# Prompt head norms in 32 rows per pair of heads beside the samples' first key group, and the prompt half of the output projection queued behind the second group's keys

## The chip, the cores and the metric

The kernel runs on one core of a Trainium2 chip. The core has a matrix engine (TensorE, PE in the profile; its weight loads are shown apart as PEld), a vector engine (VectorE, DVE), a scalar engine with function tables (ScalarE, ACT), a general engine (GpSimd, POOL) and an engine that only issues transfers (SyncE, SP). Each takes the instructions of its own queue in order and waits on semaphores for the others. TensorE writes to eight PSUM banks of 128 partitions by 512 floats; VectorE and ScalarE read them. The metric is device time of one execution in microseconds, the median of several runs.

## The reference

One step of a hybrid decoder layer for a prompt of 512 tokens and a group of 32 sample tokens (8 sequences of 4) that share the weights. The part that matters here is the end of the attention branch and the output projection:

```python
h = rmsnorm(x, w['g_mix'])
(q, kc_new, vc_new, ks_new, vs_new, kw_new, vw_new, g_nsa, xm, vm, om, i_pre, f_pre) = split_cols(h @ w['w_in'])
k_cmp = compress(kc_all, *w['cmp_k'])        # caches of 2048 tokens per sample, blocks of 32, stride 16
v_cmp = compress(vc_all, *w['cmp_v'])
o_nsa = nsa_attend(q, k_cmp, v_cmp, ks_all, vs_all, kw_all, vw_all, gates, offset, w_pre)
#   = gate0 * compressed attention + gate1 * attention over the 16 selected blocks + gate2 * window attention
o_nsa = rmsnorm(o_nsa, w['g_head_nsa'])      # over the 64 values of each of the 8 heads
hm = rmsnorm(mlstm_chunked(...), w['g_head_m']) * sigmoid(om)
mix = jnp.concatenate([o_nsa, hm], axis=-1) @ w['w_out']     # 1024 x 1024
x = x + mix
# then cross attention, SwiGLU and the final norm
```

A head norm is `y * rsqrt(mean(y*y) + 1e-6) * g`.

## The kernel before

All activations are held transposed, features on partitions and tokens on columns: 544 columns, first 512 of the prompt and then 32 of the samples. Dense products run over two column halves, `hf` 0 (columns 0 to 271) and 1 (272 to 543), so half 0 holds prompt tokens only and half 1 the rest of the prompt and all samples. A number in full precision is split into a rounded high part (ScalarE, line 213) and a remainder (VectorE or GpSimd, line 214), and a product is three matmuls (lines 218 to 220).

`oF` is [128, 8, 544]. Blocks 0 to 3 hold the attention output, two heads of 64 rows each per block; blocks 4 to 7 the mLSTM output. Once the projection's operands are split out of it, `oF` becomes `xT`, the residual stream, into which the input rows are transposed (`load_xT`, line 1811; lines 1817 and 206 or 208 in the profile).

Around the change the work comes from generators. A background generator (`compress(1)`, the compression of the values) is woven with a foreground chain `fg`: mLSTM, then `sample()`, then `open_late()`. Each step that a generator yields costs some credit, and the weave hands the other side a step when the credit is there. This sets only the order in which instructions are written down. A planner then places them on the engines' queues: it plays the program with a priced cost for each instruction, takes what is ready, and prefers what was written first. `tc.issue_after(ins)` adds an edge: the instructions of its block that run on the engine of `ins` are put behind `ins` on that engine.

`sample()` handles the samples in two groups `g` of four sequences. For each group it does the window attention; then, again for both groups, the selected keys: the compressed scores `weigh` and the choice of blocks `select`, four steps `c` in which gathered rows are turned by `keys()` (four transposes on TensorE, line 1518, and one copy by `evac`, line 206 or 208), then multiplied with the queries (`quad`, line 1528) and biased (line 1671), then the exponentials (lines 1701 and 1703). After both groups' keys come the selected values (line 1722), group 0, then group 1. The rows are gathered by indirect transfers that GpSimd issues (line 573), into eight buffers `gat`, so a gather waits until the buffer's last reader is through.

Between the values of group 0 and group 1 stands `finals_p` (line 1391), the end of the prompt's attention. For each of four blocks j it adds the compressed branch (line 1398 on TensorE, 1401 on VectorE), squares (1402, ScalarE), forms the mean over 64 rows by a product with the constant `bones` (128 x 128, two diagonal blocks of 1/64; line 1407), which leaves each mean in all 64 rows, and copies it (1408). Then one Ln (1411) and one Exp (1412) run over 128 x 2048 numbers and give the inverse root, and four VectorE instructions (1415) scale `oF`.

`finals_s` (line 1745) closes the samples; `open_late` (line 1777) splits columns 272 to 543 of `oF` for the projection (tiles `hh`, `hl`), and after the whole chain `fg` is drained, `early_mix` (line 1824) splits columns 0 to 271 (tiles `mh`, `ml`) and transposes the input rows. Only then the projection is written down (lines 1951 to 1960): half 0 with the weights' column chunks 0 and 1, then 2 and 3 (the chunks' split, `split_w`, is lines 213 and 214, tiles `whi`, `wlo`), and half 1 with chunks 2, 3, 0, 1. Chunks 0 and 1 are loaded early, one of them into a `cgat` buffer; chunks 2 and 3 pass through one `wraw` buffer (lines 1861 and 1863 on SP); chunks 0 and 1 are loaded again for half 1 into the pool `wp`, which takes over the space that `sample()` leaves. Of PSUM, the pools `psp` and `ppo` have one bank each, `ptp` and `pbd` two, `pxa` and `pxc` one.

## Time and profile before

| | |
|---|---|
| median of 3 runs | 1232.87 us (1231.31 to 1234.45) |
| profiled execution | 1243.24 us |
| its span, first to last instruction | 1241.5 us |
| TensorE busy | 1174.3 us (95%) |
| VectorE busy | 841.2 us (68%) |
| ScalarE busy | 612.4 us (49%) |
| GpSimd busy | 558.6 us (45%) |
| mean granted TensorE clock | 0.974 of full speed |
| sum of squares of the prompt's first block, line 1402 | starts at 566.5 us |
| prompt's Ln and Exp, lines 1411 and 1412 | 581.1 and 585.4 us |
| scalings, line 1415 | 587.3 to 590.1 us |

The profile is of one execution; its times count from the span's start. A row of groups gives line, engine, operation, output and input, shape, count, busy time and mean duration in nanoseconds, and the idle time before with what ended it. A row of windows gives, for a stretch, the busy time of each engine with its instructions, the granted clock, the share of the transfer engines and GB/s. A row of the chain gives start, duration and the work that was last to end at that point. Busy time of TensorE includes the latency of matmuls that overlap with nothing.

### The profile page before, as it was taken

The numbers are of one execution on the slowest core, as the hardware profiler recorded it, in microseconds if no ns is written. First come the engines' busy times: TensorE is split into PE (matmuls) and PEld (weight loads), VectorE is DVE, ScalarE is ACT, GpSimd is POOL, SyncE is SP. The second block draws the span as 40 slices with busy tenths as digits, with TensorE's granted clock in tenths as the row PEclk, the third lists the DMA queues.
The fourth block names the chain that finished last, engine by engine and source line by source line (L and its number), as shares of the span: only waits on it lengthen the run. The fifth ranks groups of instructions, "written<-read, shape, count | busy, mean of one in ns | idle before, by whom it ended". The sixth has DMA issues, their size and how long they took to land.

```text
span 1241.5 us, 24581 instructions
## 1 busy us (share of the span) xinstructions
PE 1174.3 (95%) x9220; PEld 1066.7 (86%) x9220; DVE 841.2 (68%) x1901; ACT 612.4 (49%) x1414; POOL 558.6 (45%) x686
## 2 busy tenths in 40 slices
PE   7999999899997989988999989999899999999996
PEld 5998999588885878854999987599899999999996
DVE  6337683567787687653754756554998888888874
ACT  5235665745545444466542423342665565555452
POOL 1013353566666266542342100043885576476342
PEclk9999999899997999999999998999999999999998
DMA  7324240141253185566767298630032333322411
GB/s 232 102 53 105 86 153 1 51 137 44 78 171 115 42 283 176 178 227 205 206 135 171 83 239 288 231 128 2 1 119 86 103 96 107 106 94 77 137 52 73
DMA packets 141769, 154.30 MB, mean 124 GB/s; under 512 B 17449, under 2 KB 123689, under 8 KB 141394
## 3 DMA queue, kind: packets, MB, share of 16 engines
q1 hardware_dynamic: 131922, 119.17, 32.0%
q0 software_dynamic: 9728, 33.56, 8.3%
q8 instruction: 73, 1.20, 0.4%
q14 instruction: 46, 0.38, 0.1%
HBM read 141.67 MB, written 13.12 MB: 125 GB/s over the span
## 4 chain that ended last, share of the span: by engine, by line
PE 49%; DVE 8%; ACT 3%; DMA 2%; issue 2%; SPq 1%; POOL 1%; POOLq 0%; DVEq 0%; ACTq 0%
PE xc L2291 7%; PE xa L2291 7%; PE bd L2291 5%; PE tp L2291 5%; PE bd L220 3%; PE bd L219 3%; PE bd L218 3%; DVE sp L2231 1%; DMA mkv<-in_cache_mem_k 1%; PE xa L1296 1%; PE tp L1518 1%; PE bd L2190 1%; PE xa L218 1%; PE xa L219 1%; PE xa L220 1%
## 5 line engine op out<-in xcount | busy, mean ns | idle before, releaser
L214 POOL TENSOR_TENSOR al<-fraw,ah 128x512 fp32r<-128x512 f32 (+1 forms) x104 | 127.5, 1227 | 152.4 <-ACT ah L213 124.0
L213 ACT ACTIVATE whi<-wraw 128x1024 fp32r<-128x1024 f32 (+3 forms) x74 | 62.5, 890 | 57.5 <-DMA wraw<-in_w_xv 28.2
L214 DVE TENSOR_TENSOR wlo<-wraw,whi 128x1024 fp32r<-128x1024 f32 (+3 forms) x74 | 73.6, 1026 | 19.1 <-ACT whi L213 19.0
L213 ACT ACTIVATE ah<-fraw 128x512 fp32r<-128x512 f32 (+1 forms) x112 | 65.8, 593 | 38.0 <-PE xc L2291 11.8
L218 PE MATMUL bd<-w1h,xh 128*128 128x256 f32 x256 | 82.6, 325 | 0.9 <-issue 0.9
L220 PE MATMUL bd<-w1h,xl 128*128 128x256 f32 x256 | 75.6, 298 | 3.0 <-DVE xl L214 3.0
L1198 POOL TENSOR_TENSOR xs<-xf 128x256 f32<-128x256 f32 x64 | 55.8, 878 | 50.2 <-PE xa L1296 30.5
L219 PE MATMUL bd<-w1l,xh 128*128 128x256 f32 x256 | 75.7, 297 | 0.0
L1296 PE MATMUL xa<-ws,xs 128*128 128x256 f32 x256 | 71.2, 400 | 2.4 <-DVE bq L1470 1.3
L625 POOL TENSOR_SCALAR sb<-sb,rs,gat 128x128 f32<-128x128 f32 (+3 forms) x64 | 46.1, 724 | 54.4 <-DVE rs L624 40.2
L213 ACT ACTIVATE xh<-xf 128x512 fp32r<-128x512 f32 x64 | 40.0, 629 | 45.5 <-DVE xf L1191 20.0
L213 ACT ACTIVATE ah<-sp 128x512 fp32r<-128x512 f32 (+1 forms) x64 | 35.5, 555 | 50.1 <-DVE sp L2231 22.8
L220 PEld LDWEIGHTS bd<-w1h,xl 128*128 128x128 f32 x256 | 48.9, 192 | 6.4 <-DVE xl L214 3.8
L1296 PEld LDWEIGHTS xa<-ws,xs 128*128 128x128 f32 x256 | 46.5, 201 | 8.5 <-issue 2.9
L218 PEld LDWEIGHTS bd<-w1h,xh 128*128 128x128 f32 x256 | 49.1, 193 | 5.0 <-issue 3.9
L214 DVE TENSOR_TENSOR xl<-xf,xh 128x512 fp32r<-128x512 f32 x64 | 47.5, 746 | 8.6 <-ACT xh L213 7.7
L219 PEld LDWEIGHTS bd<-w1l,xh 128*128 128x128 f32 x256 | 49.4, 193 | 4.5 <-issue 2.8
L219 PE MATMUL bd<-hlo,whi 128*128 128x272 f32 x176 | 52.0, 296 | 0.0
L218 PE MATMUL bd<-hhi,whi 128*128 128x272 f32 x176 | 51.7, 294 | 0.0
L1191 DVE STREAM_TRANSPOSE xf<-cgat 128x512 f32<-128x512 f32 x64 | 44.7, 703 | 10.2 <-POOL xs L1198 8.4
L220 PE MATMUL bd<-hhi,wlo 128*128 128x272 f32 x176 | 51.3, 292 | 0.0
L2231 DVE TENSOR_TENSOR sp<-fraw 128x512 f32<-128x512 f32 (+1 forms) x32 | 47.8, 1494 | 0.2
(990 smaller groups left out, 4667.9 us busy)
## 6 DMA issues: line engine op xcount, KB each, us to landing
fraw<-in_w_gate SPq DMA_DIRECT2D x11, 1024.0 KB
fraw<-in_w_up SPq DMA_DIRECT2D x11, 1024.0 KB
fraw<-in_w_down SPq DMA_DIRECT2D x24, 384.0 KB
mkv<-in_cache_mem_k SPq DMA_DIRECT2D x64, 128.0 KB
mkv<-in_cache_mem_v SPq DMA_DIRECT2D x16, 512.0 KB
wraw<-in_w_in SPq DMA_DIRECT2D x8, 512.0 KB
wraw<-in_w_xq SPq DMA_DIRECT2D x4, 1024.0 KB
wraw<-in_w_xk SPq DMA_DIRECT2D x4, 1024.0 KB
```

Of the source, the lines that this page charges most:

```text
L213: nc.scalar.activation(hi, src, AF.Copy)
L214: (eng or nc.gpsimd).tensor_tensor(lo, src, hi, op=OP.subtract)
L218: nc.tensor.matmul(out, ah, bh, start=first, stop=False, **kw)
L219: nc.tensor.matmul(out, ah, bl, start=False, stop=False, **kw)
L220: nc.tensor.matmul(out, al, bh, start=False, stop=last, **kw)
L625: (nc.vector, nc.gpsimd)[1].tensor_scalar(sb[:, :n], sb[:, :n], rs, gat[:, i, 3 * h + 1 + br:3 * h + 2 + br], op0=OP.mult, op1=OP.mult)
L1191: nc.vector.transpose(xf.rearrange("p a (q i) -> p q a i", q=4), gs[0].rearrange("p (q t a i) -> p t q a i", q=4, t=4, a=4)[:, t])
L1198: nc.gpsimd.tensor_tensor(xs_.rearrange("p c (v j) -> p v c j", v=2), xg[:, 0], xg[:, 1], op=OP.add)
L1296: nc.tensor.matmul(dst[2], ops[2][:, kk], w1s[t][2][:, kk], start=t == 0 and kk == 0, stop=t == 3 and kk == 1, skip_group_check=True)
L1518: nc.tensor.transpose(p[:, 128 * i:128 * i + 128], srcs(i), ident)
L2231: nc.vector.tensor_tensor(o, a, b, op=op)
L2291: nc.tensor.matmul(p[:, :HALF], w[a][:, k], x[b_][:, k], start=first and k == 0 and i == 0, stop=last and k == n - 1 and i == 2, skip_grou ...
```

## The change

`finals_p` gets a different form and a different place. Its sum of squares uses every fourth column of `bones`, so one block's result is 32 rows (16 equal rows for each of two heads) in place of 128; the four blocks stand in the four row groups of one 128 x 512 tile, and Ln and Exp run over that tile once. A matrix `spread` (formed by four small products of the same columns with the identity, and scaled by 4) brings each block's 32 rows back to 128 by a product of 32 rows, and the scaling reads that product from PSUM. The 32 rows are copied by VectorE, not ScalarE. All its PSUM banks come from the pool `ppo`. For scratch it uses `r3`, a tile of the compression's pool, the tile `SW` of the window attention, and a new tile `GX`.

The generator `fp` of it is advanced two steps after every two keys, in the first group's loop, and run to its end after that group's exponentials; the loop of the second group has the same extra yields with nothing left to do. The place between the two groups' values is gone.

`keys()` can mark its copy: the fourth key of each of the second group's steps 0, 1 and 2 is then copied by ScalarE and kept in a list `cgs["kt"]`. `early_mix` is written down before the chain `fg` is drained, with its splits behind the second mark on ScalarE; it transposes the row tiles 0 to 2 (columns 0 to 271). The split of the weights' chunks 0 and 1 stands behind the third mark. The row tiles 3 to 5 (the other columns) are transposed beside the second pair of chunks, and the loads of tiles 4 and 5 stand behind the last load of a weight chunk on SP. Row tiles 0 to 2 use only the bank of `psp`, as `ppo` is in use by the values. The pool `wp` is opened after the chain, as before.

```diff
--- before.py
+++ after.py
@@ -1388,32 +1388,36 @@
                     nc.scalar.activation(PcT[:, :, 128 * i - 128:128 * i], p[:, :256].rearrange("p (v t) -> p v t", v=2), AF.Copy)
                 yield
 
-        def finals_p(var):
+        def finals_p(sq, vt, spread):
             yield from need(("p", 1))
-            var = var[:, :2048].rearrange("p (a b n) -> p a b n", a=2, b=2)
-            for j in range(5):
-                if j < 4:
-                    acc = bank(psp)
-                    for v in range(2):
-                        nc.tensor.matmul(acc[64 * v:64 * v + 64], vcP[32 * j:32 * j + 32, v], PcT[32 * j:32 * j + 32, v],
-                                         start=True, stop=True)
-                    oj = oF[:, j, :512]
-                    nc.vector.tensor_tensor(oj, oj, acc, op=OP.add)
-                    nc.scalar.activation(var[:, j // 2, j % 2], oj, AF.Square)
-                    yield
-                if j > 0:
-                    p = bank(ptp)
-                    vj = var[:, (j - 1) // 2, (j - 1) % 2]
-                    nc.tensor.matmul(p, bones, vj, start=True, stop=True)
-                    nc.scalar.activation(vj, p, AF.Copy)
-                if j < 4:
-                    yield
-            nc.scalar.activation(var, var, AF.Ln, bias=eps_t)
-            nc.scalar.activation(var, var, AF.Exp, scale=-0.5)
+            p = bank(ppo)
             for j in range(4):
-                oj, vj = oF[:, j, :512], var[:, j // 2, j % 2]
-                nc.vector.scalar_tensor_tensor(oj, oj, gh[:, j:j + 1], vj, op0=OP.mult, op1=OP.mult)
-            yield
+                nc.tensor.matmul(p[32 * j:32 * j + 32, :128], bones[:, 0:128:4], ident, start=True, stop=True)
+            nc.scalar.activation(spread, p[:, :128], AF.Copy, scale=4.0)
+            yield
+            for j in range(4):
+                js = slice(32 * j, 32 * j + 32)
+                acc = bank(ppo)
+                for v in range(2):
+                    nc.tensor.matmul(acc[64 * v:64 * v + 64], vcP[js, v], PcT[js, v], start=True, stop=True)
+                oj = oF[:, j, :512]
+                nc.vector.tensor_tensor(oj, oj, acc, op=OP.add)
+                nc.scalar.activation(sq, oj, AF.Square)
+                yield
+                p = bank(ppo)
+                nc.tensor.matmul(p[js], bones[:, 0:128:4], sq, start=True, stop=True)
+                nc.vector.tensor_copy(vt[js], p[js])
+                yield
+            nc.scalar.activation(vt, vt, AF.Ln, bias=eps_t)
+            nc.scalar.activation(vt, vt, AF.Exp, scale=-0.5)
+            yield
+            for j in range(4):
+                js = slice(32 * j, 32 * j + 32)
+                p = bank(ppo)
+                nc.tensor.matmul(p, spread[js], vt[js], start=True, stop=True)
+                oj = oF[:, j, :512]
+                nc.vector.scalar_tensor_tensor(oj, oj, gh[:, j:j + 1], p, op0=OP.mult, op1=OP.mult)
+                yield
 
         def sample():
             yield from need(("w", 1))
@@ -1518,9 +1522,12 @@
                     nc.tensor.transpose(p[:, 128 * i:128 * i + 128], srcs(i), ident)
                 return p
 
-            def keys(srcs):
+            def keys(srcs, mark=False):
                 kt_ = sc.tile([128, 512], F32, name="kt", bufs=4)
-                evac(kt_, four_t(srcs))
+                if mark:
+                    cgs["kt"].append(nc.scalar.activation(kt_, four_t(srcs), AF.Copy))
+                else:
+                    evac(kt_, four_t(srcs))
                 return kt_
 
             def quad(S, bs, keys_of):
@@ -1536,6 +1543,7 @@
                 evac(PT_, four_t(srcs).rearrange("p (i r) -> p i r", i=4))
                 return PT_
 
+            cgs["kt"] = []
             win = {(0, "k"): kwin(0), (0, "v"): vwin(0), (1, "k"): kwin(1)}
             yield 2
             for g in range(2):
@@ -1638,6 +1646,7 @@
                 nc.vector.tensor_scalar(mk[:, 1:31], ia, -0.5 * BIG, BIG, op0=OP.is_ge, op1=OP.mult)
                 sel[g] = mk
 
+            fp = finals_p(r3, sc.tile([128, 544], F32, name="SW")[:, :512], sc.tile([128, 128], F32, name="GX"))
             G, st_ = {}, {}
             G[0, "k0"] = half("cache_k_slc", 0, 0)
             G[0, "k1"] = half("cache_k_slc", 0, 1, range(3))
@@ -1676,9 +1685,11 @@
                     kts = []
                     for q in range(4):
                         c0 = 512 * ((c + 1) % 2)
-                        kts.append(keys(lambda i: src[q][:, c0 + 128 * i:c0 + 128 * i + 128]))
+                        kts.append(keys(lambda i: src[q][:, c0 + 128 * i:c0 + 128 * i + 128], g == 1 and q == 3))
                         if q % 2:
                             yield
+                            yield next(fp, None)
+                            next(fp, None)
                     if g == 0 and c > 0:
                         (weigh, select)[c - 1](1)
                     if c == 2:
@@ -1704,6 +1715,8 @@
                 nc.vector.tensor_reduce(rs[:, 1:2], bs5[:, 5:10], axis=AX.X, op=OP.add)
                 st_[g] = SS, rs
                 yield
+                if g == 0:
+                    yield from fp
             for g in range(2):
                 SS, rs = st_[g]
                 if g:
@@ -1737,8 +1750,6 @@
                 nc.vector.tensor_tensor(rs[:, 2:3], rs[:, 2:3], g3[:, g, 1:2], op=OP.mult)
                 nc.vector.scalar_tensor_tensor(ocs[:, g], po_[:, 0:128], rs[:, 2:3], ocs[:, g], op0=OP.mult, op1=OP.add)
                 yield
-                if g == 0:
-                    yield from finals_p(sc.tile([128, 2080], F32, name="SS", bufs=2))
             pop("sc")
             pop("mixS")
 
@@ -1812,23 +1823,26 @@
             t0, n = xtl[i]
             x = xts[i]
             for c in range(2):
-                p = rot(psp, ppo)
+                p = bank(psp) if i < 3 else rot(psp, ppo)
                 for k in range(4):
                     nc.tensor.transpose(p[:, n * k:n * k + n], x[:n, 512 * c + 128 * k:512 * c + 128 * k + 128], ident[:n, :n])
                 evac(xT[:, 4 * c:4 * c + 4, t0:t0 + n], p[:, :4 * n].rearrange("p (k t) -> p k t", k=4))
 
         def close_sample():
-            load_xT(5)
-            yield
+            yield 9
+            with tc.issue_after(last_w[0].ins):
+                fetch_x((4, 5), cgat_x())
+            for i in range(3, 6):
+                load_xT(i)
+                yield
 
         def early_mix():
-            hot["wp"] = push("wp", bufs=2, side="right")
             hot[0] = [wt.tile([128, KT, HALF], R32, name=f"m{c}", bufs=1) for c in "hl"]
-            for k in (4, 5, 6, 7, 0, 1, 2, 3):
-                split(hot[0][0][:, k], hot[0][1][:, k], oF[:, k, :HALF], nc.gpsimd if k % 2 else nc.vector)
+            with tc.issue_after(cgs["kt"][1].ins):
+                for k in (4, 5, 6, 7, 0, 1, 2, 3):
+                    split(hot[0][0][:, k], hot[0][1][:, k], oF[:, k, :HALF], nc.gpsimd if k % 2 else nc.vector)
             fetch_x((2, 3), cgat_x())
-            fetch_x((4, 5), cgat_x())
-            for i in range(5):
+            for i in range(3):
                 load_xT(i)
 
         def front():
@@ -1860,7 +1874,7 @@
                 for v in range(2):
                     nc.sync.dma_start(raw[64 * v:64 * v + 64, 0:4],
                                       wo[256 * v:256 * v + 256, cs_].rearrange("(j d) c -> d j c", d=64))
-                nc.sync.dma_start(raw[:, 4:8], wo[512:1024, cs_].rearrange("(k p) c -> p k c", p=128))
+                last_w[0] = nc.sync.dma_start(raw[:, 4:8], wo[512:1024, cs_].rearrange("(k p) c -> p k c", p=128))
             return fill
 
         def wo_chunk(c):
@@ -1874,9 +1888,10 @@
         won.append((raw1,) + tuple(wt.tile([128, 2048], R32, name=f"w{x}").rearrange("p (k c) -> p k c", k=KT)
                                     for x in ("hi", "lo")))
         fetch_x((0, 1), [wt.tile([128, D], F32, name=f"xt{i}", bufs=1) for i in range(2)])
+        early_mix()
         drain(fg)
         flip[1] = 2
-        early_mix()
+        hot["wp"] = push("wp", bufs=2, side="right")
         hxp, lp, wp = hot["hx"], hot["lp"], hot["wp"]
         if stage == 5:
             drain(finals_s())
@@ -1942,13 +1957,17 @@
         mixh = from_halves(hot)
         wk = {}
 
+        def split_o(w):
+            with tc.issue_after(cgs["kt"][2].ins):
+                return split_w(w)
+
         def wo_keep(c):
             def f():
                 wk[c] = wo_chunk(c)()
                 return wk[c]
             return f
 
-        weave(chain(dense_steps([(lambda c=c: split_w(won[c]), two(2 * c)) for c in range(2)], mixh, KT, residual, dbk, group=2, hfs=(0,)),
+        weave(chain(dense_steps([(lambda c=c: split_o(won[c]), two(2 * c)) for c in range(2)], mixh, KT, residual, dbk, group=2, hfs=(0,)),
                     dense_steps([(wo_keep(c), two(2 * c)) for c in (2, 3)], mixh, KT, residual, dbk, group=2, hfs=(0,))),
               close_sample())
         wps[:] = [(hot["wp"], hot["wp"], 2, 2112)]
```

## The prediction

> **What bounds the kernel now.** I read the page first, for the engines' shares, then busy time by window around the place that the diff touches, then the groups of TensorE instructions there, the chain, and last the timeline.
>
> ```profile
> span 1241.5 us, 24581 instructions
> ...
> PE 1174.3 (95%) x9220; PEld 1066.7 (86%) x9220; DVE 841.2 (68%) x1901; ACT 612.4 (49%) x1414; POOL 558.6 (45%) x686
> ```
>
> TensorE is busy 95% of the span: the kernel is bound by it nearly everywhere, and an edit gains only where TensorE stands idle. The windows find that place.
>
> ```profile
> core 0: us, PE busy (x) PEld busy (x) DVE busy (x) ACT busy (x) POOL busy (x), PEclk, DMA share, GB/s
> 500.00:541.00 41.00, 40.37 (x328) 33.13 (x326) 26.74 (x81) 19.19 (x41) 19.37 (x24) 1.00 0.59 188
> 541.00:559.00 18.00, 12.54 (x83) 7.25 (x81) 9.48 (x20) 14.42 (x30) 9.50 (x13) 0.91 0.76 273
> 559.00:591.00 32.00, 26.51 (x343) 14.73 (x343) 13.00 (x32) 20.11 (x36) 9.67 (x9) 1.00 0.61 197
> 591.00:647.00 56.00, 55.91 (x450) 54.32 (x449) 37.60 (x76) 27.31 (x58) 23.34 (x27) 1.00 0.66 164
> ```
>
> From 500 to 541 us TensorE is full: compression of the values, with the samples' first group of keys between. From 591 to 647 it is full again: the output projection, 450 instructions in 56 us, 0.124 us each. Between lies a hole of 50 us in which weight loads fill only 7.25 + 14.73. There the second group of keys, the selected values and the prompt's head norms go one after another. Busy time flatters a thin stream, because an isolated matmul is counted with its latency; so I price the hole's work at the chain's rates. First the counts (groups of the two windows), then the rates (chain: start, us, what).
>
> ```profile
> L1518 PE MATMUL tp<-ident,gat 128*128 128x128 f32 x48 | 8.3, 310 | 1.7 <-ACT kt L206 1.5 <-DVE kt L208 0.2
> L1528 PE MATMUL sp<-kt,Qn 128*32 128x512 f32 x24 | 3.8, 709 | 3.0 <-ACT kt L206 3.0
> ...
> L1722 PE MATMUL po<-gat,PTs 128*32 128x128 f32 x224 | 10.7, 277 | 5.4 <-ACT PTs L206 3.7 <-issue 1.1 <-DVE PTs L208 0.7
> L1518 PE MATMUL tp<-ident,SS 128*128 128x128 f32 x32 | 4.9, 282 | 0.8 <-ACT whi L213 0.8
> L1407 PE MATMUL tp<-SS,bones 128*128 128x512 f32 x8 | 4.5, 644 | 0.0
> L1398 PE MATMUL sp<-PcT,vcP 32*64 32x512 f32 x16 | 4.3, 612 | 0.0
> L1722 PE MATMUL po<-cgat,PTs 128*32 128x128 f32 x32 | 2.1, 276 | 0.0
> L1528 PE MATMUL sp<-kt,Qn 128*32 128x512 f32 x8 | 1.1, 604 | 0.0
> ```
>
> ```profile
> 505.39 0.87 PE tp L1518 x8
> ...
> 537.02 0.99 PE sp L1528 x8
> ...
> 566.71 1.00 PE sp L1398 x4
> 567.72 1.22 PE po L1722 x32
> 568.93 1.05 PE tp L1407 x2
> ...
> 581.12 2.00 ACT SS L1411
> 583.12 0.97 ACT PTs L206 x2
> 584.11 1.28 ACT L1412
> 585.40 1.92 ACT SS L1412
> 587.34 2.74 DVE oF L1415 x4
> ```
>
> 541 to 559: 48 transposes at 0.87/8 are 5.2, 24 score instructions at 0.99/8 are 3.0, and 1.0 for small groups left out (an estimate at the same rates): 9.2 of 18, so 8.8 idle. 559 to 591: 256 value instructions at 1.22/32 are 9.8, 32 transposes 3.5, eight of L1407 4.2, sixteen of L1398 4.0, eight scores 1.0, small groups 2.5: 25.0 of 32, so 7.0 idle. **The hole holds 15.8 us of idle TensorE**, and 8.2 us of its work (L1398, L1407) are the prompt norms. It ends by them: Ln, a table load, Exp and four scalings one after another, and behind the first scaling the projection's first matmul, at 588.94 in the timeline (start, us, engine, line, output<-inputs; in brackets idle time before and what ended it):
>
> ```profile
> 554.04 1.06 ACT L213 ACTIVATE whi<-wraw 128x1024 fp32r<-128x1024 f32 x1
> ...
> 556.62 1.22 DVE L214 TENSOR_TENSOR wlo<-wraw,whi 128x1024 fp32r<-128x1024 f32 x1
> ...
> 562.91 0.09 PEld L1727 LDWEIGHTS tp<-ident,SS 128*32 128x32 f32 x1 [0.20 <-issue]
> ...
> 575.52 0.19 PEld L1398 LDWEIGHTS sp<-PcT,vcP 32*64 32x64 f32 x4 [0.76 <-DVE oF L1401]
> ...
> 583.65 1.08 PE L1722 MATMUL po<-gat,PTs 128*32 128x128 f32 x32 [3.14 <-ACT PTs L206]
> ...
> 588.94 0.37 PE L218 MATMUL xa<-mh,whi 128*128 128x272 f32 x1
> ...
> 590.12 0.43 ACT L213 ACTIVATE mh<-oF 128x272 fp32r<-128x272 f32 x1 [0.23 <-DVE oF L1415]
> ...
> 592.22 0.35 DVE L1738 SCALAR_TENSOR_TENSOR po<-po,rs,po 128x128 f32<-128x128 f32 x1
> ...
> 606.54 1.26 SPq L1861 DMA_DIRECT2D wraw<-in_w_out  x2
> ...
> 611.30 1.06 ACT L213 ACTIVATE whi<-wraw 128x1024 fp32r<-128x1024 f32 x1 [2.89 <-DMA wraw<-in_w_out]
> ...
> 613.54 0.86 DVE L214 TENSOR_TENSOR hl<-oF,hh 128x32 fp32r<-128x32 f32 x2
> ...
> 620.75 0.44 DVE L1897 TENSOR_TENSOR oF<-oF,bd 128x272 f32<-128x272 f32 x1 [2.21 <-PE bd L220]
> ...
> 646.65 0.44 DVE L1897 TENSOR_TENSOR oF<-oF,bd 128x272 f32<-128x272 f32 x1 [0.54 <-PE bd L220]
> ```
>
> The projection's first half is done at 620.75, its second at 646.65. The first half, columns 0 to 271, holds prompt tokens alone: 8 blocks x 8 k x 3 are 192 instructions, 23.8 us at 0.124. It needs nothing of the samples, and yet nearly all of it comes after 591.
>
> **The change, part by part.**
>
> *Norms moved.* Out of the hole go 8.2 us of TensorE, four adds and scalings on VectorE, and on ScalarE four squares, four copies, Ln (2.00) and Exp (1.92). Beside the first group come: four score-value products, 4.0 as before; four sums of squares with 32 rows out; a small product that forms the spread matrix, about 0.4; four spreads of 32 rows back to 128. Two of these are not in the trace. A 32-row sum is bounded by 0.25 (a quarter of an L1528 group, which runs four side by side) and 1.05 (L1407); I take 1.05, since nothing runs beside it. A spread is bounded by 0.5 (half an L1398 group) and 1.25 (L1407 and the 0.20 of row 562.91); I take 1.05, since one bank keeps the four apart. In all 4.0 + 4.2 + 0.4 + 4.2 = 12.8, **4.6 more than before** (bounds: 2.3 less, 5.4 more), and it lands where TensorE has 0.6 us free. Nothing hides it there; it pushes compression to the right, into the 8.8 idle us. The Trainium skill, "TensorE: Matmul & The Clock Gate", section Part 2, speaks against the change: a matmul's time is that of the columns streamed, so 32 rows out in place of 128 save nothing. By that rule the sums stay at 4.2; by the lower row they would be 1.0 and the gain 3.2 us more; no row here has such a sum alone.
>
> ScalarE gets cheaper (512 columns through Ln and Exp, not 2048: some 2.7 us less, and no copies). VectorE takes four copies of some 0.7, at 26.7 busy of 41: I cost them at nothing; were it not free, each would hold the norms' one bank for as long.
>
> *Mix splits behind the second mark, weight splits behind the third.* The weight splits (four of 1.06 from 554.04) leave the second group's keys alone, but four more mix splits of 0.43 come in. Queued behind the waiting splits on ScalarE are the first group's probabilities and copies of prompt rows; TensorE waits for both. The first weights are ready no sooner than two splits and a remainder after the last key: 2.1 + 1.2 = 3.3.
>
> *Projection's first half into the hole.* From about 560 on TensorE has 25.0 - 8.2 = 16.8 us of sample work left, and 23.8 of projection to put between.
>
> *Queues.* On SP the last row tiles now stand behind the third and fourth chunk of the weights. Their buffer comes free only at the samples' last values, as before, so they lose nothing. The fourth chunk took 4.8 us (606.54 to 611.30) under other matmuls; in the hole it shares the DMA with the value gathers: 1 to 2 us of stall. On POOL four remainders of the mix stand among the gathers; their data is there by the second mark, so I add no wait.
>
> **The sum.** From 500 to 647 TensorE holds the same work plus 4.6, and the end moves by idle time removed less work added. All of the hole filled: 15.8 - 4.6 = 11.2. What stays idle I put at 5: 3.3 before the first weights, some 1 at the fourth chunk, some 1 of keys that wait for ScalarE. Bounds: 1, about what the full stages show, and 14, nearly all of the hole. So **6.2 us come out**. The second half does not wait: it is reached at about 620.75 - 6.2 = 614.5; the samples' last value came at 592.22 and its split columns followed at 613.54 only because nothing needed them sooner, and with no Ln and Exp ahead of their probabilities (3.14 at 583.65) they come earlier. All later work follows the second half, so the shift lasts to the end. The profiled execution took 1243.24 us, 1.74 around its span, and becomes 1237.0. It lay 10.4 above the runs' median, 1232.87, which becomes **1226.7**.
>
> **Rivals.**
>
> *The hole is filled wholly*, 1 us stays idle. For it: with three sources of work the planner left 0.63 us idle in 41. Against: a mark, a split and a load stand in a row at the hole's middle. 15.8 - 4.6 - 1 = 10.2: 1222.7.
>
> *Shape changes eat it.* Each norm group has another array shape than compression, and the rows show 0.20 before such a group (562.91). Twelve groups in and out are 24 x 0.20 = 4.8 more in a full stage: 6.2 - 4.8 = 1.4, 1231.5. Against: score groups change the shape too, and 0.99 by the chain is all they cost. The Trainium skill, "TensorEngine Tiling (Array Packing)", section Key Properties, says that a change of tiling mode drains TensorE; by that rule this rival is right, and the 0.20 agrees with it.
>
> *The projection stays behind the samples.* TensorE takes its queue in order. If the projection is queued behind the second group's values, which wait for gathers, only Ln, Exp and scalings leave the hole's end (about 6), while 12.8 of norms, less 8.8 of idle, come in before it and the first weights cost 2: 1233. Against: ready work is placed first.
>
> *Slower: the norms stall the full stage.* Each pair of heads goes TensorE, VectorE, ScalarE, TensorE, VectorE through one bank, between 500 and 545. In the hole this chain held TensorE 0.76 at a hop (575.52). If it does so at twelve hops, 9.1 of stalls join the 4.6 of work; the second group comes 20 us late, its gathers with it, and the hole gives back only half, 8: +5.7, 1238.6. It decides once the stalls and what they leave unfilled pass 6.2, half a microsecond a hop. Against: the 0.63 of idle, though chains as long run there already.
>
> **How the numbers follow.** Forecast 0.48, own range 1222 to 1229.5; filled wholly 0.16; shape changes 0.12; behind the samples 0.10; slower 0.14. A measurement of this kernel tells 0.3%, 3.7 us, from no change. Faster by more (below 1229.2): 0.46 of the forecast, 0.16, and 0.02 of the shape changes: 0.64. Within: 0.02, 0.09, 0.09, 0.02 of the last: 0.22. Slower: 0.01, 0.01 and 0.12: 0.14. The range runs from 1217, the filled hole with the sums and spreads near their lower bounds, to 1239, the slower rival.
>
> **What would show it.** Right: no Ln of 2048 columns near 581; scalings before the second group's last keys; projection matmuls (L218 to L220 with mh) among the selected values; compression's last matmul 8 to 13 us later; the second half some 6 us earlier. Over 3 us of idle TensorE before 541 speaks for the stalls, 0.2 at each norm group for the shapes. I am wrong if compression's end moves less than 5 us, or if TensorE idles over 10 us between the last key and the second half.

## The result, and the profile after

The kernel became **slower**: 1250.2 us (median of four, 1247.9 to 1253.3) against 1233.7, a ratio of 1.0128 (1.0102 to 1.0153), 16.5 us. I had put 1226.7, and a range that ended at 1239.

The profile of before that the prediction used came from an execution 10 us above its own median. The same kernel was profiled a second time (run e0 below), in an execution of 1235.7 us. In it the first group's first score product and the second half's last residual, which bound the stage of the change, stand here (timeline: start, us, engine, line):

```profile
504.17 1.05 PE L1528 MATMUL sp<-kt,Qn 128*32 128x512 f32 x4
...
640.70 0.44 DVE L1897 TENSOR_TENSOR oF<-oF,bd 128x272 f32<-128x272 f32 x1 [0.54 <-PE bd L220]
```

and in the changed kernel, whose profiled execution took 1249.0, here:

```profile
506.10 1.06 PE L1535 MATMUL sp<-kt,Qn 128*32 128x512 f32 x8
...
652.55 0.43 DVE L1912 TENSOR_TENSOR oF<-oF,bd 128x272 f32<-128x272 f32 x1
```

The stage takes 136.5 us before (136.6 in the first profile, from 510.0) and 146.4 after: **9.9 us longer**. The spans differ by 13.2 (1234.0, 1247.2). Of the other 3.3, 1.9 lie ahead of the stage (506.10, not 504.17) and 1.4 behind it, so these profiles place some 10 us of the 16.5; where the rest lies is not shown. The windows of the changed kernel, over the stretches the prediction used:

```profile
500.00:541.00 41.00, 41.00 (x278) 28.66 (x276) 25.28 (x63) 17.99 (x37) 13.82 (x18) 1.00 0.49 153
541.00:559.00 18.00, 13.78 (x55) 6.88 (x52) 7.85 (x26) 11.29 (x23) 2.77 (x6) 0.75 0.50 167
559.00:591.00 32.00, 29.11 (x210) 18.89 (x209) 14.93 (x26) 17.03 (x37) 12.09 (x14) 0.82 0.57 181
591.00:647.00 56.00, 53.66 (x574) 49.81 (x573) 33.93 (x78) 25.62 (x57) 20.93 (x26) 1.00 0.70 194
```

The hole did fill: by shown busy time TensorE idles 9.5 us over these four windows, against 11.7 before (12.7 in the second profile). But the column behind POOL, the granted clock, reads 0.75 and 0.82 where it read 0.91 and 1.00. 18 x 0.25 + 32 x 0.18 are 10.3 us of lost TensorE time, against 1.6 before. TensorE's own rows show where it begins:

```profile
540.09 1.07 PE L1535 MATMUL sp<-kt,Qn 128*32 128x512 f32 x8
...
541.67 1.08 PE L1408 MATMUL po<-r,bones 128*32 128x512 f32 x2
542.68 1.09 PE L1522 MATMUL tp<-ident,gat 128*128 128x128 f32 x8
544.61 1.09 PE L1522 MATMUL tp<-ident,gat 128*128 128x128 f32 x8 [0.84 <-DVE kt L208]
548.70 0.65 PE L1522 MATMUL tp<-ident,gat 128*128 128x128 f32 x4 [3.00 <-ACT kt L206]
549.74 2.01 PE L1417 MATMUL po<-SW,GX 32*128 32x512 f32 x2 [0.38 <-ACT SW L1412]
551.67 1.97 PE L1246 MATMUL xc<-w,hid 128*127 128x64 f32 x8
...
555.58 1.94 PE L1535 MATMUL sp<-kt,Qn 128*32 128x512 f32 x8
...
570.97 1.07 PE L1535 MATMUL sp<-kt,Qn 128*32 128x512 f32 x8 [0.17 <-ACT kt L1528]
```

A score group takes 1.07 at 540, 1.94 at 555 and 1.07 again at 571. Between lies the half clock, and ahead of it TensorE stands still for 3.0 us because it waits for ScalarE to copy a transposed key (kt). ScalarE's rows say why the copy is late:

```profile
543.81 0.60 ACT L206 ACTIVATE kt<-tp 128x512 f32<-128x512 f32 x1 [0.51 <-PE tp L1522]
544.42 1.28 ACT L1411 ACT_TABLE_LOAD   x1
545.72 0.72 ACT L1411 ACTIVATE SW<-SW,eps_t 128x512 f32<-128x512 f32 x1
546.46 1.28 ACT L1714 ACT_TABLE_LOAD   x1
547.75 0.32 ACT L1714 ACTIVATE SS<-sn,nmn 128x32 f32<-128x32 f32 x1
...
548.07 0.57 ACT L206 ACTIVATE kt<-tp 128x512 f32<-128x512 f32 x1
...
549.07 0.62 ACT L1412 ACTIVATE SW<-SW 128x512 f32<-128x512 f32 x1
```

Ln of the norms needs a table of its own. It is loaded, used for 0.72 us, and another is loaded for the exponential behind it, all between two key copies. And because TensorE takes its queue in order, the second group's first score product at 555.58 stands behind two spreads (L1417) that wait for Exp.

Behind the stage the memory attention changes. These are its two groups of TensorE instructions, of before (second profile) and of after:

```profile
L2091 PE MATMUL po<-mkv,Qx 128*32 128x256 f32 x128 | 11.0, 384 | 0.0
L2140 PE MATMUL po<-mkv,Qx 128*32 128x256 f32 x128 | 10.0, 385 | 0.0
```

```profile
L2159 PE MATMUL po<-mkv,Qx 128*32 128x256 f32 x128 | 13.7, 386 | 0.0
L2110 PE MATMUL po<-mkv,Qx 128*32 128x256 f32 x128 | 9.6, 383 | 0.2 <-DVE mkv L2120 0.2
```

One group of 128 instructions takes 3.7 us more and the other 1.4 less, 2.3 more in all. In the longer one the changed order of the program leaves smaller runs of them, and a run of two takes as long as a run of six (timeline, before then after):

```profile
784.11 0.63 PE L2140 MATMUL po<-mkv,Qx 128*32 128x256 f32 x6
```

```profile
797.45 0.62 PE L2159 MATMUL po<-mkv,Qx 128*32 128x256 f32 x2
```

From the second half's last residual to the end the kernel before took 594.4 and 592.9 us in its two profiles, the changed kernel 594.2 and 598.1 (here and in run e11), so a loss behind the stage is not clear of the scatter.

### The profile page after: what moved, and what is told of

Read it like the earlier page. It is cut to its first block, busy times and chain, and to the rows that moved or that the text cites. A ratio compares the mean times of both kernels' runs of the same rounds, so it can differ in the third digit from the quotient of the medians.

```text
span 1247.2 us, 24627 instructions
## 1 busy us (share of the span) xinstructions
PE 1185.8 (95%) x9236; PEld 1070.9 (86%) x9236; DVE 834.3 (67%) x1902; ACT 611.0 (49%) x1414; POOL 562.6 (45%) x686
## 4 chain that ended last, share of the span: by engine, by line
PE 54%; DVE 6%; DMA 5%; issue 3%; POOL 2%; ACT 1%; SPq 1%; POOLq 0%; DVEq 0%; ACTq 0%
PE xc L2310 7%; PE xa L2310 7%; PE bd L2310 6%; PE tp L2310 5%; PE bd L219 3%; PE bd L218 3%; PE bd L220 3%; PE xa L1296 2%; PE tp L1522 2%; DMA wraw<-in_w_xv 2%; PE bd L2209 1%; PE po L2159 1%; DMA r<-in_cmp_w_v 1%; PE sp L1535 1%; PE xa L218 1%
## 5 line engine op out<-in xcount | busy, mean ns | idle before, releaser
L213 ACT ACTIVATE ah<-po 128x512 fp32r<-128x512 f32 (+1 forms) x64 | 35.7, 557 | 23.2 <-PE xa L2310 13.8
```

What stands on the lines that cost most here:

```text
L213: nc.scalar.activation(hi, src, AF.Copy)
```

## The experiments

Each run was timed against the kernel before on the same chip; ratios are to it, with 95% intervals. One hundredth is 12.3 us. "Half clock" is the time an execution spends at half the TensorE clock, worked out from its mean granted clock: (1 - clock) x 2 x span.

The theories, by the letters that the expectations use. A: the stillness behind Ln's table loads halves the clock, and that is nearly the whole loss. B: the second group's keys and gathers are late by their place in the queues. C: the norms' products in the full stage make the keys late, and these set the end. D: the early projection itself holds up the samples. R and S, of the half clock behind the stillness: it stays because of the spreads' 32 rows (R), or whatever the rows (S). Q: the second group's keys are late because they stand behind spreads that wait for Exp.

**e0, the kernel before again.** No edit.

> The kernel before, unchanged, for a second look at its stages, because its profiled execution (1243.2 us) lies 10 us above its median (1233). If those 10 us were lost ahead of the stage of the change, the stage from 500 to 647 us has here the same length as in the first profile and the work ahead of it is 5 to 10 us shorter; if they were lost inside the stage, the hole of 50 us behind the compression is here shorter by that much.

Measured: 1235.7. The stage is as long as in the first profile. Of the 7.5 us between the two spans 5.9 are there when the stage begins (510.05, 504.17) and none arises in it, so the stage's rows in the prediction stand.

**e11, the changed kernel again.** No edit.

> The changed kernel once more, for the share of halved clock in each of its executions beside those of the three runs above on the same chip. Theory A: its executions spend 70 to 85 us at half clock and those of the kernel before 45 to 65; the time grows by half a microsecond for each microsecond so spent, between kernels as between executions of one kernel.

Measured: 1249.2, ratio 1.0123 (1.0092 to 1.0155). Its executions spend 70 to 77 us at half clock (72 to 82 in the first four), those of before on this chip 47 to 59. The other half of the expectation, half a microsecond of time for each at half clock, is seen most plainly among the executions of e3 below: 67 us go with 1238.5 and 1240.6, 82 with 1248.1. The four of e11 do not show it by themselves: 70 go with 1251.4 and 77 with 1247.4.

**e3, the norms moved, the projection where it was.**

```diff
-        early_mix()
         drain(fg)
         flip[1] = 2
-        hot["wp"] = push("wp", bufs=2, side="right")
+        early_mix()
```

Row tiles, splits and the functions around them are those of before as well.

> The kernel before with the norms in 32 rows beside the first group, and the projection where it was, behind the samples. Theory A: the same table loads stand among the second group's keys, the clock halves again, and the norms alone cost 5 to 10 us: 1238 to 1243. Theory B in the form that the early projection's splits, loads and products hold up the samples: the norms alone are no slower than before, 1228 to 1236. My prediction's own price for the norms was 4.6 us of TensorE work saved from the hole: with the projection behind the samples that is a gain of up to 7 us, 1226 to 1233.

Measured: 1243.7, ratio 1.0078 (1.0049 to 1.0107). The move of the norms alone makes the kernel slower, with the same stillness (2.99 us) and 67 to 82 us of half clock against 47 to 59. My price for it, a gain of up to 7 us, is wrong; the early projection is not the main cause. In the profiles the stage is as long as the changed kernel's (146.2, 146.4); behind it the two groups of the memory attention take 19.8 us together and not 23.3, over half of the 0.5% between the two kernels.

**e4 and e5, both kernels without products and norms.**

```diff
             yield from need(("p", 1))
+            for _ in range(10):
+                yield
...
```

In place of all that the function did stand empty turns, 14 in the changed kernel.

> The kernel before without the prompt's compressed products and norms (its output lacks them; turns and all else as before). Together with the next run it gives the price of the norms in each place and the worth of the early projection without them. The norms' TensorE work in the old place is 8.2 us, and TensorE idles 12 to 16 us in that stretch in both profiles of the kernel before. Theory C (the samples' chain of keys, scores, exponentials and values sets the end of the stage, and the old norms lie in its gaps): leaving them out saves less than 5 us, 1228 to 1233. Theory A and my prediction (TensorE's work sets it): up to 8 us, 1224 to 1229.

> The changed kernel without the prompt's compressed products and norms (its output lacks them; the early projection and all turns stay). Theory C: the norms' 12.8 us in the full stage ahead of 541 us held the first group's keys 8 us and the second group's 17 us; without them the keys come as in the kernel before, and the time falls by 15 us or more, to 1225 to 1235, at or under the previous run's. Theory D (the early projection itself holds up the samples): the time stays over 1240 and clearly above the previous run's.

Measured: 0.9977 (0.9956 to 0.9998) and 0.9971 (0.9951 to 0.9991). So the norms cost 0.23%, **2.9 us, in the old place**, and 1.0128 - 0.9971 = 1.57%, **19 us, in the new**; the early projection without them is worth 0.06%, nothing that can be measured: theory D falls. The two profiles show why so little: the early projection makes the stage 2.9 us shorter (131.4, 128.5) and the memory attention 4.3 longer (19.8, 24.1). e5 is also a bound: even with norms that cost nothing this change, as its program is ordered, would be only 0.3% faster.

**e1, the stillness filled.** Three products that nobody reads, behind the second group's first transposes.

```diff
             nc.scalar.activation(vt, vt, AF.Exp, scale=-0.5)
+            f = bank(ppo)
+            for _ in range(3):
+                nc.tensor.matmul(f, bones, sq, start=True, stop=True)
             yield
```

> The changed kernel with three idle products of 128x512 (3.1 us of TensorE work whose result nobody reads) put behind the second group's first transposes, where TensorE stood still for 3.0 us while ScalarE loaded tables for Ln and Exp. Theory A (that stillness halves the clock for 20 us): the granted clock from 541 to 591 us stays near 1.0 where the changed kernel had 0.75 and 0.82, the second group's spreads and score products take 1.0 us and not 2.0, and the time falls by 7 to 10 us, to 1240 to 1243. Theory B (the second group's keys and gathers are late by their place in the queues, and the clock stretches only work that would have waited for them): the time stays within 3 us of the changed kernel's 1250.

Measured: 1251.2, ratio 1.0162 (1.0124 to 1.0201): no gain. In the profiled execution the half clock came only in single windows of 3.4 us, and that was also the fastest, 1245.7; the others, 1249.7 to 1254.4, spent 77 to 83 us at half clock. Filling one hole with 3.1 us of work neither holds the clock reliably nor pays for itself. This speaks against theory A in its simple form.

**e6, Ln and Exp left out.**

```diff
-            nc.scalar.activation(vt, vt, AF.Ln, bias=eps_t)
-            nc.scalar.activation(vt, vt, AF.Exp, scale=-0.5)
```

> The changed kernel without the two operations Ln and Exp of the norms (its output has squares' means in place of inverse roots); the two table loads go with Ln, and every product, sum and spread stays. Theory A (the loads' 3.0 us stillness and the halved clock that follows): the clock stays near 1.0 and the time falls by 7 to 10 us to 1240 to 1243. Theory C (the keys were late already by the norms' products): it falls by the 3 us of the hole and not more than 6, 1244 to 1247, even if the clock is full.

Measured: 1239.8, ratio 1.0011 (0.9984 to 1.0038), half clock 47 to 62 us in nine of ten executions. **1.17%, 14 us, hang on these two operations**, more than either theory allowed. In the two profiles the stage is 11.1 us shorter (135.4, 146.4): 4.2 us less idle time, and some 7 of clock. The windows show the clock full through 559:

```profile
541.00:559.00 18.00, 17.31 (x105) 9.20 (x103) 10.70 (x33) 10.25 (x24) 6.52 (x10) 1.00 0.70 233
559.00:591.00 32.00, 28.24 (x282) 21.07 (x275) 17.69 (x29) 18.21 (x36) 13.48 (x15) 0.89 0.70 223
```

The products, sums and spreads that are still there cost 1.0011 - 0.9971 = 0.40%, 5 us (1 to 9 by the intervals). That is their price in the new place, and not the 4.6 of the prediction, which was a difference of two places; less the 2.9 of the old place, some 2 us stand beside it.

**e9, an idle Ln in the kernel before.**

```diff
+                    if c == 3 and g == 0:
+                        nc.scalar.activation(sc.tile([128, 544], F32, name="SW")[:, :512], SS[:, 1536:2048], AF.Ln, scale=0.0, bias=1.0)
```

> The kernel before with one idle Ln of 512 columns behind the first group's last score product, whose result nobody reads: two table loads and 0.7 us on ScalarE at the place where the changed kernel has them, and nothing else of the change. Theory A: the loads alone cost most of the loss, 7 to 14 us (ratio 1.006 to 1.011), with a stillness of TensorE of some 3 us near 540 and windows of half clock behind it. Theory C (the norms' products cost it, and the loads only add to keys that are late anyway): at most 3 us, ratio under 1.0025.

Measured: ratio 1.0025 (1.0008 to 1.0043), 3 us. Two loads stand among the key copies as in the changed kernel,

```profile
532.38 1.28 ACT L1674 ACT_TABLE_LOAD   x1
533.67 0.63 ACT L1674 ACTIVATE SW<-SS 128x512 f32<-128x512 f32 x1
...
534.49 1.28 ACT L1705 ACT_TABLE_LOAD   x1
```

and cost a fifth of what leaving out Ln and Exp saves. The loads alone are not it; theory A falls in this form too. The place is not quite the same: TensorE's longest stillnesses behind these loads were 1.55 and 2.18 us, not 3.0, and no product of 32 rows stood among the keys.

**e8 and e2, the inverse root elsewhere.** e8 forms it on VectorE, e2 on GpSimd:

```diff
-                nc.vector.tensor_copy(vt[js], p[js])
+                nc.vector.tensor_scalar(vt[js], p[js], EPS, None, op0=OP.add)
...
-            nc.scalar.activation(vt, vt, AF.Ln, bias=eps_t)
-            nc.scalar.activation(vt, vt, AF.Exp, scale=-0.5)
+            ki = sq.bitcast(I32)
+            nc.vector.tensor_scalar(ki, vt.bitcast(I32), 1, None, op0=OP.logical_shift_right)
+            nc.vector.tensor_scalar(ki, ki, -1.0, 1597463007.0, op0=OP.mult, op1=OP.add)
+            t_ = bank(ppo)
+            for _ in range(2):
+                nc.vector.scalar_tensor_tensor(t_, sq, -0.5, sq, op0=OP.mult, op1=OP.mult)
+                nc.vector.tensor_tensor(t_, t_, vt, op=OP.mult)
+                nc.vector.scalar_tensor_tensor(sq, t_, 1.5, sq, op0=OP.add, op1=OP.mult)
...
-                nc.tensor.matmul(p, spread[js], vt[js], start=True, stop=True)
+                nc.tensor.matmul(p, spread[js], sq[js], start=True, stop=True)
```

```diff
-            nc.scalar.activation(vt, vt, AF.Ln, bias=eps_t)
-            nc.scalar.activation(vt, vt, AF.Exp, scale=-0.5)
+            nc.vector.tensor_scalar(vt, vt, EPS, None, op0=OP.add)
+            nc.gpsimd.tensor_tensor(vt, vt, mhalf[:, 0:1].to_broadcast([128, 512]), op=OP.pow)
```

> The changed kernel with the norms' inverse square root formed on VectorE (a shifted integer as first guess and two Newton steps, eight operations of 128x512) in place of Ln and Exp: the output is whole, and ScalarE loads no table among the keys. Theory A (the loads cost nearly all: stillness behind them, then TensorE at half clock): the time comes down to that of the run without Ln and Exp, a ratio of 1.000 to 1.004 to the kernel before, and the granted clock from 541 to 591 us is near 1.0. If VectorE's eight operations (some 5 us) hold the keys as the loads did, the ratio stays over 1.007.

> The changed kernel with the norms' inverse square root formed on GpSimd (one power over 128x512) and not by Ln and Exp on ScalarE: both table loads (2 x 1.28 us) and 1.3 us of ScalarE's work leave the queue of key copies. Theory A: the hole of 3.0 us in TensorE goes, the clock stays near 1.0 to 591 us, and the time falls by 7 to 10 us to 1240 to 1243, unless the power itself takes more than about 4 us on GpSimd, whose queue also forms the second group's masks: then the spreads come late by what is above that. Theory B: within 3 us of 1250.

Measured: e8 1250.0, ratio 1.0126 (1.0098 to 1.0155); e2 1322.4, because the power took

```profile
544.69 82.44 POOL L1412 TENSOR_TENSOR SW<-SW,mhalf 128x512 f32<-128x512 f32 x1 [5.92 <-DVE nmn L1708]
```

and says nothing of the question. e8 says something: no table is loaded, the clock is 1.00 from 541 to 559 and 0.95 to 591, the second group's keys are only some 7 us late (last score product at 561.4, 554.0 in e0), and nothing is gained. The second half stands still later instead, with the clock halved there (0.87 from 591 to 607, 0.92 to 647):

```profile
602.65 0.42 PE L1834 MATMUL sp<-ident,cgat 16*128 16x16 f32 x4 [1.37 <-ACT oF L206]
604.58 0.98 PE L1834 MATMUL po<-ident,cgat 112*128 112x112 f32 x4 [1.50 <-DMA cgat<-in_x_prompt]
617.79 0.33 PE L1782 MATMUL tp<-ident,po 128*128 128x128 f32 x1 [2.81 <-DVE po L1778]
```

TensorE waits there for row tiles that the change queues behind the samples, and for a late step of the samples. So it may be that part of e6's gain is the chain from sums to spreads, shorter there by a whole link, and not only the tables that are gone; no run shows this link by itself.

**e7 and e10, the norms held until the first group's last score product**; e10 with e8's inverse root besides.

```diff
-                            yield next(fp, None)
-                            next(fp, None)
...
-                for v in range(2):
-                    nc.tensor.matmul(acc[64 * v:64 * v + 64], vcP[js, v], PcT[js, v], start=True, stop=True)
+                with tc.issue_after(cgs["q"][3].ins):
+                    for v in range(2):
+                        nc.tensor.matmul(acc[64 * v:64 * v + 64], vcP[js, v], PcT[js, v], start=True, stop=True)
```

`cgs["q"][3]` is the first group's last score product.

> The changed kernel with the norms taken out of the first group's turns and held until the first group's last score product, so that they lie among the second group's keys, in the stretch in which TensorE idled; projection early as in the change. Theory C: the first group's last score product is again at about 532 us after a start of that group at 504 (541 in the changed kernel), the second group's are at most 6 us later than in the kernel before, and the time is 1228 to 1238. Theory A: Ln's two table loads now fall among the second group's last keys or the values, and if they still TensorE for over 2 us the clock halves there too: 1240 or more. Theory D: over 1245.

> Both cures at once: norms held until the first group's last score product, their inverse root on VectorE, projection early as in the change. Neither the first group's keys nor the table loads are in the way of anything. If what is left of the change's thought is right (prompt work fills the samples' gaps), this is at or under the kernel before: a ratio of 0.996 to 1.001. If the second group's keys are as late as with the norms held and Ln kept (1.0115), the norms' work among these keys is the cost, and not the tables: over 1.006.

Measured: 1.0115 (1.0077 to 1.0152) and 1.0191 (1.0155 to 1.0228). The first group's keys are back on time: from its first to its last score product 26.5 us in e7 (510.8 to 537.3), 26.9 in e0, 34.0 in the changed kernel. The second group's last comes 54.1 us behind the first product, 49.8 in e0 and 70.9 in the changed kernel. And yet nothing is gained: timely keys alone do not bring the end forward, which speaks against theories C and B. TensorE now walks the norms' end in order, in front of the values:

```profile
564.92 1.93 PE L1536 MATMUL sp<-kt,Qn 128*32 128x512 f32 x8 [2.45 <-ACT kt L1529]
568.05 1.22 PE L1418 MATMUL po<-SW,GX 32*128 32x512 f32 x2
575.34 2.07 PE L1418 MATMUL po<-SW,GX 32*128 32x512 f32 x2 [5.05 <-DVE oF L1420]
```

It stands still for 2.45 and for 5.05 us, and behind each it runs at half clock for a while (1.93 for a score group, 2.07 for a spread); between, at 568.05, a spread took 1.22.

**e12, spreads of 128 rows.** TensorE's order in this kernel is the changed kernel's, instruction for instruction; four of them use four times the rows, and two scalings of VectorE change places.

```diff
-                nc.tensor.matmul(p, spread[js], vt[js], start=True, stop=True)
+                nc.tensor.matmul(p, spread, vt, start=True, stop=True)
```

> The changed kernel with the four spreads taken over all 128 rows and not over 32 (each then holds a mixture of the four pairs, so the output is not the reference's; order, columns and every other instruction are those of the change). In both profiles of the changed kernel the half clock began with the stillness of 3.0 us behind Ln's table loads and lasted 20.5 us, though TensorE is shown nearly full from 549 on; the kernel before had stillnesses of 2.6 to 3.1 us there too, and 3.4 us of half clock. Theory R (work of 32 rows does not count as enough for the clock to come back): with 128 rows the half clock ends within 7 us of its start, and the time falls by 4 to 7 us, to a ratio of 1.006 to 1.010. Theory S (rows do not matter; the clock stays down for what else stands there, transposes and 32-column score products): still 14 to 20 us of half clock and a ratio of 1.010 to 1.015.

Measured: ratio 1.0070 (1.0050 to 1.0090), **0.5 to 0.6% less than the changed kernel, 6 to 7 us, for the rows alone** (some 3 to 10 by the intervals; the changed kernel itself was not run on this chip). In the profiles the stage is 6.9 us shorter (139.6, 146.4). The same stillness is followed by a short half clock:

```profile
553.45 1.12 PE L1522 MATMUL tp<-ident,gat 128*128 128x128 f32 x4 [2.99 <-ACT kt L206]
554.49 2.07 PE L1417 MATMUL po<-SW,GX 128*128 128x512 f32 x2
...
557.96 1.45 PE L1417 MATMUL po<-SW,GX 128*128 128x512 f32 x2
559.34 1.07 PE L1535 MATMUL sp<-kt,Qn 128*32 128x512 f32 x8
```

The windows, of the changed kernel and then of e12, put side by side how long it lasts:

```profile
549.00:570.40 21.40, 21.02 (x66) 9.79 (x65) 6.75 (x14) 7.33 (x18) 3.90 (x4) 0.52 0.38 129
```

```profile
552.00:559.00 7.00, 5.55 (x16) 3.60 (x16) 1.70 (x4) 6.01 (x16) 1.28 (x2) 0.52 0.77 280
559.00:571.00 12.00, 10.24 (x65) 5.00 (x64) 7.49 (x12) 6.43 (x15) 5.42 (x6) 1.00 0.46 145
```

With 32 rows TensorE is shown busy for 21.02 of 21.40 us and stays at half clock all the while; with 128 it is back after 7. Theory R holds.

**e13, the spreads behind the second group's second score product.**

```diff
-                    quad(S, bs, lambda q: kts[q])
+                    w = quad(S, bs, lambda q: kts[q])
...
+                    if g == 1 and c == 1:
+                        with tc.issue_after(w.ins):
+                            scale_p(*nt)
```

`scale_p` holds the four spreads and scalings, without their yields.

> The changed kernel with the spreads and scalings held until the second group's second score product; Ln and Exp stay where they were, and the output is whole. In the changed kernel the second group's first score product stood behind two spreads that waited for Exp, in TensorE's own order. Theory Q (that order makes the keys late, and with them masks, gathers and values): the second group's first score product comes some 5 us sooner after the first group's last (14.4 us there in the changed kernel, 6.4 in the kernel before), its last too, and the time falls by 4 to 8 us, ratio 1.006 to 1.010. Theory R: spreads no longer follow the hole, so the half clock is short as well, and the time falls by up to 10 us. If neither holds, that is if what is won here is given back by a later first weight and later row tiles of the projection, as with the Newton steps, the ratio stays over 1.010.

Measured: 1.0072 (1.0046 to 1.0098), 6 to 7 us less than the changed kernel. The first score product of the second group comes 13.0 us behind the first group's last (556.64 less 543.68, start to start) and not 15.5 (555.58 less 540.09; the 14.4 above counts from its end), half of the 5 us that Q named, and spreads of 32 rows no longer follow the stillness:

```profile
556.64 1.94 PE L1536 MATMUL sp<-kt,Qn 128*32 128x512 f32 x8 [1.13 <-ACT kt L206]
562.21 1.16 PE L1536 MATMUL sp<-kt,Qn 128*32 128x512 f32 x8
563.30 1.12 PE L1419 MATMUL po<-SW,GX 32*128 32x512 f32 x2
```

They take 1.12 here, at full clock. Behind the stillness the half clock still lasts some 10 us (a granted clock of 0.57 over the 12.00 us from 551.00), between e12's 7 and the changed kernel's 20.5. Both theories gave this time. The profile leans to the clock (R): the stage is 3.8 us shorter (142.6, 146.4), of which the windows give some 3.3 to the clock and 0.3 to idle time; the other 3 us of the gain it does not place.

## Why the prediction was wrong

**The part that failed is "Norms moved".** I priced it at 4.6 us of TensorE work. Left out in both places, the norms cost 2.9 us in the old one and 19 in the new (e4, e5), so the move cost 16 (some 5 either way by the intervals), as much as the whole loss. Two things were missing from the price, the two operations on ScalarE and the clock; they overlap, so their figures below do not add up.

**TensorE's added work: right.** I had 12.8 us of norms beside the keys, 4.6 more than in the old place. In the changed kernel's profile the products took 4.3, the sums 4.3 and the spread matrix 0.5. The spreads took 8.2 at half clock, two instructions in 1.12 at full clock (e13), so 4.5 for the four. Sums and spreads came out near the 1.05 that I chose for each; the lower bound, 2.3 us less than before, counts one spread and not four, with which it is 0.8 less. The rule that I weighed there, of the Trainium skill's "TensorE: Matmul & The Clock Gate", Part 2, agrees: 32 rows saved nothing.

**The full stage took that work without stalls: right.** TensorE is busy 41.00 of 41 us to 541. The rival of stalls, 0.76 at a hop, named a slower kernel by a mechanism that did not occur, so that its sign came true says nothing for it. The rival of shape changes falls too. Its 0.20 was read in front of a transposition of the samples' probabilities (562.91), which has the 128 x 32 shape of the values ahead of it, so no shape changes there; the product at 538.27 and the dense work behind it show no idle time, so these rows don't show the drain of the Trainium skill's "TensorEngine Tiling (Array Packing)", Key Properties. Compression's last matmul came 9 us later, counted from the first group's first score product (539.62 less 506.10, against 528.58 less 504.17), inside my 8 to 13:

```profile
528.58 0.28 PE L220 MATMUL bd<-w1h,xl 128*128 128x256 f32 x1
```

```profile
538.27 1.07 PE L1402 MATMUL po<-PcT,vcP 32*64 32x512 f32 x4
539.27 0.39 PE L218 MATMUL bd<-w1h,xh 128*128 128x256 f32 x1
...
539.62 0.28 PE L220 MATMUL bd<-w1h,xl 128*128 128x256 f32 x1
```

**"ScalarE gets cheaper": the step of it that failed.** I counted Ln and Exp by their columns, 2.7 us less on an engine that is half idle, and took the sign from that. I did not name what is queued behind them on ScalarE in the new place, and gave no price there to a table load, though one stood in the old chain that I quoted (584.11, 1.28). In the old place the two loads held up the norms and little else (2.9 us for all of the norms, e4). In the new one they stand between two key copies for which TensorE waits; e6 prices the two operations there at 14 us. That this is the loads alone is not shown: an idle Ln with two loads cost 3 us (e9), and without any load, but with eight operations on VectorE instead, nothing was gained (e8).

**The clock: left out of the sum.** I valued the hole at full clock before and after. In the changed kernel the clock takes 8.7 us more than before (10.3 less 1.6), the largest term in the stage. e12 takes 6 to 7 us of time away by one property of the change, spreads of 32 rows behind a stillness. The Trainium skill, "TensorE: Matmul & The Clock Gate", section Part 1, has the clock come back after one busy window of some 3.4 us; the row from 549.00 to 570.40 doesn't agree, with 21.02 of 21.40 us busy and 0.52 granted; e12's rows, at full clock again 5.9 us after the stillness ended (559.34 less 553.45), come nearer to it.

**Idle time: 15.8 to 5 was too hopeful.** By the windows' busy time it went from 11.7 to 9.5, and without any norms, in e5, to 9.2. The rest was neither the first weights nor the fourth chunk that I named, but ScalarE's key copies (3.00 at 548.70, where I had allowed 1), VectorE's (2.47 at 575.10) and the last value gather, 9.91 us from issue to landing, for which TensorE idled 1.84:

```profile
575.10 1.09 PE L1522 MATMUL tp<-ident,gat 128*128 128x128 f32 x8 [2.47 <-DVE kt L208]
...
595.53 9.91 DMA gat<-in_cache_v_slc,gx
605.48 1.98 PE po L1735 x62
```

**"All later work follows the second half": right within the scatter.** The end moved with the stage. The memory attention did change with the early projection: its two groups took 23.3 us together in the changed kernel and in e12, 23.5 in e6 and 24.1 in e5, against 19.8 in e3 and 21.0 in the kernel before.

Of the 9.9 us by which the stage grew, the clock is 8.7 and idle time takes back 2.2, which leaves 3.4 for the added work (4.4 by the second profile's idle time), where I had 4.6. So the work was sized about right, the idle time was not won, and the clock had no term. My signs of failure (compression's end, idle time over 10 us behind the last key) would not have shown it: both came out as forecast. Of the signs of being right, the second half 6 us earlier is the one that failed.

**What stays open.** How the 14 us of e6 divide between the stillness, the clock and the shorter chain: its profile has 4.2 less idle time and some 7 less clock in the stage, but not what caused each. e9 gives 3 for two loads without 32-row work behind them, e12 and e13 give 6 to 7 each and share the clock, and e8 shows that the gain can be given back further down. Some 6 of the 16.5 us lie outside the stage, and no run says where. Why one stillness of some 3 us is followed by half clock and another is not (in e0 one of 3.14 at 577.57 was not) no run here settles.

## What to carry to other kernels

When an operation is moved, ask on its own engine what it now stands in front of, table loads included: off the path in the old place says nothing of the new. A gap in TensorE can cost more than its length by what follows it, so read the granted clock beside the busy share; here helper products of 128 rows in place of 32, behind such a gap, were worth 6 to 7 us. Price each part of a change by leaving it out, in both places: here that showed in two runs that the early projection won 2.9 us in its stage and gave them back behind it.

## What the runs showed of the hardware

- Being busy did not bring the TensorE clock back from half: with four spreads of 32 rows among transposes and 32-column products, TensorE was busy for 21.02 of 21.40 us and had 20.5 us of half clock behind the stillness. With 128 rows and the same order it had 6.8 (e12), without the spreads some 10 (e13). At full clock spreads of 32 rows did not bring it down: in e6 the same four stand among the keys from 547 to 557, with 1.00 granted up to 559.
- Products of 32 columns overlap where they stand together: two of L2159 took 0.62 us, six of L2140 0.63.
- Ln and the exponential behind it loaded a table each, 1.28 us.
- A power over 128x512 on GpSimd took 82.44 us, 0.16 a column.
